# A three-stage fp32 trunk on one core: HGRN2's squares go into used-up keys, the last two features are made token-major by blocks, and the first weights are loaded ahead of x

## The chip, the cores and the metric

The kernel runs on one core of a Trainium2 chip. The time is that of the device for one execution, in microseconds; before the change it is 1544.46, the median of three runs (1542.48 to 1546.43). One execution was profiled; it took 1544.98. The engines are TensorE (PE: matrix products and transposes), VectorE (DVE), ScalarE (ACT), GpSimd (POOL) and SyncE (SP), which issues nearly all DMA transfers.

## The reference, cut to what matters

The input is x, 512 tokens of 1024 features in float32. Layer 0 mixes tokens with HGRN2 (8 heads of 128), layer 1 with Mamba-2 (a state-space mixer); each is followed by a gated convolutional feed-forward stage (2816 wide, "ConvGLU"). Every stage adds to a residual stream h, and a last RMSNorm ends it.

```python
def hgrn2_mixer(u, w_in, lb, norm_w, w_out):
    q, f_fw, f_bw, iv, g = jnp.split(u @ w_in, 5, axis=-1)
...
    o = gla_chunked(q, k_fw, iv, logf_fw) + flip(gla_chunked(flip(q), flip(k_bw), flip(iv), flip(logf_bw)))
    o = rmsnorm(o, norm_w) * jax.nn.silu(heads(g))
    return o.reshape(bsz, seq, HG_DIM) @ w_out
```

So the output of a head is normalised by the mean of its 128 squares per token, multiplied by a gate, and projected. The last line of the whole is rmsnorm(h, final_norm_w): for each token, the 1024 features divided by the root of their mean square, times a weight per feature.

## The kernel before

**Layout.** Nearly everything lies feature-major: 128 features on the partitions, 512 tokens along them; h is 8 such tiles. Weights come from memory in pieces of 128 x 4 x 256 floats (`load`, L123 to L131). `halves` (L133) splits each into a rounded half `whi`, cast by ScalarE (L137), and a rest `wlo`, subtracted by VectorE (L138); activations are split into `uhi`, `ulo` in the same way. `mm3` (L162) makes a product of high precision from three: hi x hi, hi x lo, lo x hi (L163 to L165). These triples are most of TensorE's work: 512 or 256 columns each, 128 x 128 stationary.

**HGRN2 (up to about 350 us).** The projections of the 8 heads, two heads at a time (`proj_pair`), and then the output projection are the "fill": a generator that reports how many units it has issued (a triple of 256 columns is about half a unit). `mix` (L544) is a head's attention, cut by `yield` into steps: five levels that both heads of a pair take together, then four steps for each head apart: transposes of keys (`kt`), states (`sd`, L653), output (`po`, L670), and transposes of the normalised output (L683). `weave` runs the fill and takes a step of a head when the fill has issued as many units as three tables say: a pair's start, its levels, and the ends of its first and second head, counted from the pair's start.

```python
PAIRS = (66, 138, 214, 289)
LEVELS = (0, 5, 18, 32, 45)
ENDS = ((50, 55, 62, 69), (56, 61, 68, 74))
```

That is TensorE's order, which is written out by hand. VectorE, ScalarE and GpSimd get theirs from a scheduler that places what is ready by the order of the program. Behind the output product stands a head's end, in the step L670 to L688: four squares on ScalarE with the sums of each row (L674, into `on`), the mean on VectorE (L675), a power on GpSimd (L677), four scalings on ScalarE (L679, `po` to `on`); in the last step four transposes on TensorE (L683), gate (L685, `on`), `yhi` on ScalarE, and `ylo` on VectorE (L687), the last reader of `on`. `on` has one buffer for all heads. `kq` holds a head's keys and queries, forward and backward, in four planes (KF, QB, QF, KB), in two buffers; the plane KF is last read by the transposes of the keys. The next pair's `kq`, its sum of keys (`km`, L596) and the gates F (L514) stand between these on VectorE; TensorE's first step of the next pair needs that `km` of both heads.

**The start (L327 on).** SyncE issues x in four pieces of 128 tokens and the first weights in turn. TensorE transposes each piece of x (L407), 8 transposes for each; between them, on ScalarE and VectorE, the first weights and the features are split.

**The end (`last_out`, L1109).** The last projection makes two feature tiles (256 features) from each of four pieces of weights, 10 triples of 512 columns for a tile; the last piece is done in two halves of 256 columns. `finish` adds the product to h, squares it and sums over the tiles, scales by the norm weight, and one tile later transposes 128 x 128 blocks to token-major `o`; after the last tile come the sums over features (`stats`, L223), a power on GpSimd (L234), the scaling of o by `rtok` on VectorE (L1132) and ScalarE, and two transfers for each block of 128 tokens (L1135).

## Time and profile before

| | |
|---|---|
| median of three runs | 1544.46 us |
| the profiled execution | 1544.98 us |
| its span in the trace | 1543.2 us |
| mean granted clock of TensorE, share of full | 0.995 |
| instructions | 24667 |
| busy: TensorE, VectorE, ScalarE, GpSimd | 99%, 67%, 51%, 2% |

The span is the time from the first to the last instruction that the profile shows; the execution's own time has 1.8 us around it. A granted clock of 1.00 is TensorE's upper level, 2.4 GHz; 0.50 is the lower, 1.2 GHz. A row of the timeline gives start, duration, engine, line, operation, tiles written and read, and in brackets how long the engine had been idle before and what ended that. TensorE's instructions overlap: one of 128 x 512 is shown at 0.39 us, and the next starts 0.23 us after it.

### The profile page before, as it was taken

To read this page: it belongs to the slowest core of one execution; us is meant where nothing else is said; L and a number is where in the kernel's file an instruction comes from. 1 tells how busy PE (TensorE), PEld (TensorE's weight loads), DVE (VectorE), ACT (ScalarE), POOL (GpSimd) and SP (SyncE) were. 2 spreads that over 40 slices of the span, in tenths; PEclk is the share of its full clock that TensorE was granted. 3 is DMA by queue.
4 is the path that set the end of the run, shared out by engine and by line. 5 is a ranking of instruction groups with operands and counts; after the bars stand their busy time and mean duration, and the time that the engine had idled before them with its cause. 6 is when DMAs were issued, how large, how long until landed. Compare 5 with 4: busy or idle time off the path is not lost.

```text
span 1543.2 us, 24667 instructions
## 1 busy us (share of the span) xinstructions
PE 1521.1 (99%) x9959; PEld 1289.5 (84%) x9959; DVE 1035.1 (67%) x1675; ACT 794.1 (51%) x1418; POOL 26.5 (2%) x31
## 2 busy tenths in 40 slices
PE   9999999999999999999999999999999999999998
PEld 7888888887888888888888888888888888888887
DVE  6887777748665346554999987788877665346542
ACT  5656555445433223333699888668745432223333
POOL 0000000000000000000000000000000000000000
PEclk9999999999999999999999999999999999999999
DMA  6321221113232233223454443343213232233221
GB/s 198 96 80 59 70 70 62 57 48 123 96 98 94 94 97 110 77 95 102 101 164 127 143 123 110 102 132 109 83 62 123 96 100 92 96 96 110 79 91 63
DMA packets 153593, 151.52 MB, mean 98 GB/s; under 512 B 8375, under 2 KB 144264, under 8 KB 153480
## 3 DMA queue, kind: packets, MB, share of 16 engines
q1 hardware_dynamic: 153415, 149.93, 31.2%
q8 instruction: 78, 1.28, 0.3%
q14 instruction: 36, 0.29, 0.1%
q0 software_dynamic: 32, 0.02, 0.0%
q10 hardware_dynamic: 32, 0.01, 0.0%
HBM read 147.70 MB, written 2.23 MB: 97 GB/s over the span
## 4 chain that ended last, share of the span: by engine, by line
PE 88%; ACT 4%; DVE 4%; DMA 2%; issue 1%; POOL 1%; SPq 0%; POOLq 0%; ACTq 0%; DVEq 0%
PE pp L163 25%; PE pp L164 25%; PE pp L165 25%; PE pm L165 1%; PE pm L163 1%; PE pm L164 1%; ACT E L952 1%; PE pm L561 1%; PE pm L974 1%; PE pm L1007 1%; PE pm L670 1%; PE pm L1022 1%; DVE wlo L138 1%; PE pm L653 1%; DMA raw<-in_b_w_in_dram 1%
## 5 line engine op out<-in xcount | busy, mean ns | idle before, releaser
L163 PE MATMUL pp<-uhi,whi 128*128 128x512 f32 x1136 | 450.6, 397 | 0.9 <-ACT sz L905 0.9
L165 PE MATMUL pp<-uhi,wlo 128*128 128x512 f32 x1136 | 443.0, 390 | 0.0
L164 PE MATMUL pp<-ulo,whi 128*128 128x512 f32 x1136 | 442.6, 390 | 0.0
L137 ACT CAST whi<-raw 128x1024 fp32r<-128x1024 f32 (+1 forms) x258 | 259.2, 1007 | 293.2 <-PE pp L164 223.7
L138 DVE TENSOR_TENSOR wlo<-raw,whi 128x1024 fp32r<-128x1024 f32 (+1 forms) x258 | 301.2, 1169 | 134.2 <-ACT whi L137 133.7
L163 PEld LDWEIGHTS pp<-uhi,whi 128*128 128x128 f32 x1136 | 213.6, 188 | 45.3 <-ACT sz L905 1.3
L165 PEld LDWEIGHTS pp<-uhi,wlo 128*128 128x128 f32 x1136 | 213.4, 188 | 45.6 <-DVE wlo L138 0.4
L164 PEld LDWEIGHTS pp<-ulo,whi 128*128 128x128 f32 x1136 | 213.7, 188 | 43.0 <-issue 0.2
L163 PE MATMUL pp<-yh,whi 128*128 128x512 f32 (+1 forms) x500 | 194.3, 389 | 0.0
L165 PE MATMUL pp<-yh,wlo 128*128 128x512 f32 (+1 forms) x500 | 190.6, 381 | 0.0
L164 PE MATMUL pp<-yl,whi 128*128 128x512 f32 (+1 forms) x500 | 190.4, 381 | 0.0
L163 PE MATMUL pp<-whi,uhi 128*128 128x256 f32 x384 | 112.2, 292 | 0.0
L164 PE MATMUL pp<-wlo,uhi 128*128 128x256 f32 x384 | 110.2, 287 | 0.0
L165 PE MATMUL pp<-whi,ulo 128*128 128x256 f32 x384 | 110.1, 287 | 0.0
L165 PEld LDWEIGHTS pp<-yh,wlo 128*128 128x128 f32 x500 | 94.0, 188 | 18.3
L163 PEld LDWEIGHTS pp<-yh,whi 128*128 128x128 f32 x500 | 94.0, 188 | 17.9 <-DVE h L268 0.3
L164 PEld LDWEIGHTS pp<-yl,whi 128*128 128x128 f32 x500 | 94.1, 188 | 17.4
L268 DVE TENSOR_TENSOR h<-h,pp 128x512 f32<-128x512 f32 x80 | 54.3, 684 | 79.8 <-PE pp L165 79.3
L952 ACT ACTIVATE E<-R,col_t 128x128 f32<-128x128 f32 x256 | 81.7, 394 | 7.2 <-DVE E L956 4.9
L727 ACT ACTIVATE c<-gp,colp 128x512 f32<-128x512 f32 x44 | 35.7, 816 | 89.8 <-DVE gp L725 89.8
L729 DVE SCALAR_TENSOR_TENSOR c<-gp,colp,c 128x512 f32<-128x512 f32 x88 | 65.6, 750 | 18.9 <-ACT c L727 17.5
L163 PEld LDWEIGHTS pp<-whi,uhi 128*128 128x128 f32 x384 | 75.4, 196 | 0.6
(281 smaller groups left out, 1974.9 us busy)
## 6 DMA issues: line engine op xcount, KB each, us to landing
raw<-in_ffn_w_in_dram SPq DMA_DIRECT2D x88, 512.0 KB, 3.5
raw<-in_a_w_in_dram SPq DMA_DIRECT2D x40, 512.0 KB, 3.6
raw<-in_ffn_w_out_dram SPq DMA_DIRECT2D x40, 512.0 KB, 3.4
raw<-in_b_w_in_dram SPq DMA_DIRECT2D x32, 512.0 KB, 4.0
R<-ac_d SPq DMA_DIRECT2D x64, 256.0 KB, 3.6
raw<-in_b_w_in_dram SPq DMA_DIRECT2D x32, 256.0 KB, 4.0
raw<-in_b_w_out_dram SPq DMA_DIRECT2D x12, 512.0 KB, 3.4
xt<-in_x_dram SPq DMA_DIRECT2D x4, 512.0 KB, 8.3
```

Source lines behind the costliest of these rows:

```text
L137: A.copy(hi[:, :nk, :c0], r)
L138: V.tensor_tensor(lo[:, :nk, :c0], r, hi[:, :nk, :c0].bitcast(F32), ALU.subtract)
L163: PE.matmul(dst, lhi, rhi, start=start, stop=False)
L164: PE.matmul(dst, lhi, rlo, start=False, stop=False)
L165: PE.matmul(dst, llo, rhi, start=False, stop=stop)
L268: V.tensor_tensor(h[d], h[d], p, ALU.add)
L561: PE.matmul(p[j:j + Q, b * Q:(b + 1) * Q], lhs(b * P + j), rhs(b * P + j), start=True, stop=True)
L653: PE.matmul(pl[:, n * P:(n + 1) * P], kt[dr][:, n * P:(n + 1) * P], v[:, b, i * P:(i + 1) * P], start=True, stop=True)
L670: PE.matmul(po[:, ts], l, r, start=n == 0, stop=n == len(parts) - 1)
L727: A.activation(c, g[:, 0:T], AF.Identity, scale=col(W_FW[l], f), bias=col(W_FB, l * NFF + f))
L729: V.scalar_tensor_tensor(c, g[:, k:k + T], col(W_FW[l], k * NFF + f), c, ALU.mult, ALU.add)
L952: A.activation(e[:, bs], r[:, bs], AF.Identity, bias=col_t[:, b, dr * NH + hd:dr * NH + hd + 1])
```

## The change

There are four edits. The table ENDS gives the first head's last two steps and the second head's last three earlier places (one or two units), so that two pairs of steps change places on TensorE. In `mix`, the squares are written into the plane KF of the head's own `kq`; only the scaling writes to `on`. At the start, the first weights are loaded ahead of x, and split ahead of the first transposed column table. And `last_out` makes the last two tiles in another way: for each block of 128 tokens the activations are the stationary side and 256 columns of weights are moved, so that the product comes out token-major; h of these two tiles is transposed into `o` at the beginning of the stage, the sums over the first six tiles are made ahead, and `close` ends each block by itself: add, squares with their sum per token, mean, power, scaling, two transfers. The last 256 norm weights are loaded over all partitions once (`wl`) by GpSimd.

```diff
--- before.py
+++ after.py
@@ -34,7 +34,7 @@
-ENDS = ((50, 55, 62, 69), (56, 61, 68, 74))
+ENDS = ((50, 55, 61, 67), (56, 61, 67, 74))
...
+    def sums():
         pst = misc_ps()
-        for b in blocks:
-            for n, s in enumerate((ssum, *more)):
-                for j in range(0, P, Q):
-                    PE.matmul(pst[j:j + Q, b:b + 1], s[:, b * P + j:b * P + j + Q], ones[:, 0:1],
-                              start=n == 0, stop=n == len(more))
-        bs = slice(blocks[0], blocks[-1] + 1)
+        for b in range(NB):
+            for j in range(0, P, Q):
+                PE.matmul(pst[j:j + Q, b:b + 1], ssum[:, b * P + j:b * P + j + Q], ones[:, 0:1], start=True, stop=True)
+        return pst
+
+    def stats(tmp):
+
+        pst = sums()
         ms = tmp.tile([P, NB], F32, tag="ms", name="ms", bufs=2)
-        V.tensor_scalar(ms[:, bs], pst[:, bs], 1.0 / D, EPS, ALU.mult, ALU.add)
-        G.tensor_tensor(rtok[:, bs], ms[:, bs], nhalf[:, bs], ALU.pow)
+        V.tensor_scalar(ms, pst[:, 0:NB], 1.0 / D, EPS, ALU.mult, ALU.add)
+        G.tensor_tensor(rtok, ms, nhalf, ALU.pow)
@@ -324,10 +323,10 @@
         nc.sync.dma_start(rows[r:r + n, g, :], src)
         return (g, r)
-    load_x(0)
     parts = [plan.popleft()[1] for _ in range(4)]
     raws = [None] * 4
     raws[0] = load(parts[0])
+    load_x(0)
     load_x(1)
     raws[2] = load(parts[2])
     load_x(2)
@@ -424,12 +423,12 @@
         for _ in range(16):
             PE.transpose(pt[:, P:2 * P], ident, ident)
         first_masks()
+        w = halves(*raws[0])
         PE.transpose(pt[:, :16], n1, ident[:16, :16])
         V.tensor_copy(coln, pt[:, :16])
         come(0, 1, 2, 3)
         split(0, W_N1, px[0])
         split(1, W_N1, px[1])
-        w = halves(*raws[0])
         first_products(0, 0, 2, w)
         stay(0, 1)
         come(4, 5)
@@ -668,10 +667,11 @@
                 parts += [(kq[:, a, ts], states[dr, t]) for dr, a in ((0, QF), (1, QB)) if (dr, t) in states]
                 for n, (l, r) in enumerate(parts):
                     PE.matmul(po[:, ts], l, r, start=n == 0, stop=n == len(parts) - 1)
-            on = t2k("on", 1)
+
+            on, sq = t2k("on", 1), kq[:, KF, :]
             ss = pool.tile([P, NB], F32, tag="ss", name="ss", bufs=2)
             for t in range(NB):
-                A.activation(on[:, t * P:(t + 1) * P], po[:, t * P:(t + 1) * P], AF.Square, accum_out=ss[:, t:t + 1])
+                A.activation(sq[:, t * P:(t + 1) * P], po[:, t * P:(t + 1) * P], AF.Square, accum_out=ss[:, t:t + 1])
             V.tensor_scalar(ss, ss, 1.0 / P, EPS, ALU.mult, ALU.add)
             rs = pool.tile([P, NB], F32, tag="rs", name="rs", bufs=2)
             G.tensor_tensor(rs, ss, nhalf, ALU.pow)
@@ -1109,50 +1109,74 @@
     def last_out(key, yhi, ylo, pool):
         o = [pool.tile([P, D], F32, tag="o", name="o", bufs=NB) for _ in range(NB)]
-        nk, po = len(yhi), [None]
-        def finish(d, p, ts, blocks):
-            V.tensor_tensor(h[d][:, ts], h[d][:, ts], p[:, ts], ALU.add)
-            sq = squares(d, pool, ts, d < ND - 1)
-            A.activation(h[d][:, ts], h[d][:, ts], AF.Copy, scale=col(W_FN, d))
+        wl = pool.tile([P, 256], F32, name="wl")
+        nc.gpsimd.dma_start(wl, final_norm_w[D - 256:D].rearrange("(a c) -> a c", a=1).to_broadcast([P, 256]))
+        nk, po, last = len(yhi), [None], 6
+        ms1, ms, sqt = (pool.tile([P, NB], F32, name=n) for n in ("ms1", "msl", "sqt"))
+        def finish(d, p):
+            V.tensor_tensor(h[d], h[d], p, ALU.add)
+            squares(d, pool)
+            A.activation(h[d], h[d], AF.Copy, scale=col(W_FN, d))
             to = po[0]
             yield
-            if d == ND - 1:
-                stats(pool, blocks, (sq,))
-            for b in blocks:
-                PE.transpose(to[b][:, d % 4 * P:(d % 4 + 1) * P], h[d][:, b * P:(b + 1) * P], ident)
-            if d == ND // 2 - 1:
-                for b in blocks:
-                    A.copy(o[b][:, 0:D // 2], to[b])
-            if d == ND - 1:
-                lo, hi = slice(0, D // 2), slice(D // 2, D)
-                for b in blocks:
-                    r = rtok[:, b:b + 1]
-                    V.tensor_scalar(o[b][:, lo], o[b][:, lo], r, None, ALU.mult)
-                    A.activation(o[b][:, hi], to[b], AF.Copy, scale=r)
-                    for ds in (lo, hi):
-                        nc.sync.dma_start(out[0, b * P:(b + 1) * P, ds], o[b][:, ds])
+            for b in range(NB):
+                t = to[b][:, d * P:(d + 1) * P] if d < 4 else to[b // 2][:, b % 2 * 256 + d % 2 * P:b % 2 * 256 + d % 2 * P + P]
+                PE.transpose(t, h[d][:, b * P:(b + 1) * P], ident)
+            if d == 3:
+                for b in range(NB):
+                    A.copy(o[b][:, 0:512], to[b])
+            if d == last - 1:
+                for b in range(NB):
+                    A.copy(o[b][:, 512:768], to[b // 2][:, b % 2 * 256:b % 2 * 256 + 256])
+                pst = sums()
+                V.tensor_scalar(ms1, pst[:, 0:NB], 1.0 / D, EPS, ALU.mult, ALU.add)
+        def close(b, p):
+            r, bs, hi = rtok[:, b:b + 1], slice(b, b + 1), o[b][:, 768:D]
+            V.tensor_tensor(hi, hi, p[:, 0:256], ALU.add)
+            sq = pool.tile([P, 256], F32, tag="sql", name="sql", bufs=2)
+            A.activation(sq, hi, AF.Square, accum_out=sqt[:, bs])
+            V.scalar_tensor_tensor(ms[:, bs], sqt[:, bs], 1.0 / D, ms1[:, bs], ALU.mult, ALU.add)
+            G.tensor_tensor(r, ms[:, bs], nhalf[:, bs], ALU.pow)
+            V.tensor_scalar(o[b][:, 0:512], o[b][:, 0:512], r, None, ALU.mult)
+            A.activation(o[b][:, 512:768], o[b][:, 512:768], AF.Copy, scale=r)
+            V.scalar_tensor_tensor(hi, hi, r, wl, ALU.mult, ALU.mult)
+            for ds in (slice(0, 512), slice(512, D)):
+                nc.sync.dma_start(out[0, b * P:(b + 1) * P, ds], o[b][:, ds])
         left = iter(())
         with tc.manual_schedule(engines={mybir.EngineType.PE}):
-            for c in range(4):
+            for b0 in (0, 2):
+                pt = misc_ps()
+                for b in (b0, b0 + 1):
+                    for i in range(2):
+                        t = (b - b0) * 256 + i * P
+                        PE.transpose(pt[:, t:t + P], h[last + i][:, b * P:(b + 1) * P], ident)
+                for b in (b0, b0 + 1):
+                    A.copy(o[b][:, 768:D], pt[:, (b - b0) * 256:(b - b0) * 256 + 256])
+            for c in range(3):
                 w = take((key, c))
-                if c % 2 == 0:
-                    po = [[misc_ps() for _ in range(NB)]]
-                for n in range(1 if c < 3 else 2):
-                    blocks = range(NB) if c < 3 else range(2 * n, 2 * n + 2)
-                    ts = slice(blocks[0] * P, (blocks[-1] + 1) * P)
-                    for i in range(2):
-                        p = proj_ps()
-                        for k in range(nk):
-                            mm3(p[:, ts], w(0, k, i * P), w(1, k, i * P), yhi[k][:, ts], ylo[k][:, ts],
-                                k == 0, k == nk - 1)
-                            if k == nk // 2:
-                                run(left)
-                        left = finish(2 * c + i, p, ts, blocks)
-                        next(left)
-            run(left)
+                if c != 1:
+                    po = [[misc_ps() for _ in range(NB if c == 0 else 2)]]
+                for i in range(2):
+                    p = proj_ps()
+                    for k in range(nk):
+                        mm3(p, w(0, k, i * P), w(1, k, i * P), yhi[k], ylo[k], k == 0, k == nk - 1)
+                        if k == nk // 2:
+                            run(left)
+                    left = finish(2 * c + i, p)
+                    next(left)
+            w = take((key, 3))
+            for b in range(NB):
+                bs = slice(b * P, (b + 1) * P)
+                p = proj_ps()
+                for k in range(nk):
+                    mm3(p[:, 0:256], yhi[k][:, bs], ylo[k][:, bs], w(0, k, 0, 256), w(1, k, 0, 256), k == 0, k == nk - 1)
+                    if k == nk // 2:
+                        run(left)
+                close(b, p)
     hgrn2()
     ffn(0, lambda key, yh, yl, pool: run(out_proj(key, yh, yl, lambda d: prep(d, (W_N1[0], W_N1[1] + 8), pool))))
```

On TensorE, around the end of the third pair (heads 4 and 5; `at_2425` is the first head's, `at_2436` the second's), before, from the first head's states to the second head's output:

```order
L653 MATMUL pm<-v,kt 128x128 x6
L670 MATMUL pm<-v,at_2425 128x128
...
L670 MATMUL pm<-v,at_2436 128x128
...
L165 MATMUL pp<-uhi_86,wlo 128x512
L683 MATMUL pm<-ident,on 128x128 x4
...
L165 MATMUL pp<-uhi_90,wlo 128x512
L683 MATMUL pm<-ident,on 128x128 x4
```

And now (lines have moved by one):

```order
L669 MATMUL pm<-v,at_2425 128x128
...
L652 MATMUL pm<-v,kt 128x128 x6
...
L165 MATMUL pp<-uhi_84,wlo 128x512
L683 MATMUL pm<-ident,on 128x128 x4
L669 MATMUL pm<-v,at_2436 128x128
...
L165 MATMUL pp<-uhi_90,wlo 128x512
L683 MATMUL pm<-ident,on 128x128 x4
```

Before, the second head's output stands ahead of the first head's transposes, with six products between them, and 12 products lie between the two sets of transposes. Now the first head's transposes come directly ahead of the second head's output, and 18 products lie between that and the second set; the first head's output comes ahead of the second head's states.

On VectorE, at the same place, before (`ss_3235` is the second head's sum of squares, `kq_3322` and `km_3329` are the next pair's second head's):

```order
L511 TENSOR_TENSOR pr_3281<-pp_3216,rbc_99 128x512
L138 TENSOR_TENSOR wlo_3295<-raw_3292,whi_3294 128x1024
L675 TENSOR_SCALAR ss_3235<-ss_3235 128x4
L514 TENSOR_SCALAR F_2954<-pr_3281,olb_107,lb_106 128x512
L552 TENSOR_TENSOR kq_3322<-q_2952,F_2954 128x512
L685 SCALAR_TENSOR_TENSOR on_3234<-pm_3273,colp_102,g_2775 128x512
L596 TENSOR_TENSOR km_3329<-kq_3322 128x512
L687 TENSOR_TENSOR ylo5_505<-on_3234,yhi5_497 128x512
```

And now (`ss_3243` and `on_3242` are the second head's):

```order
L675 TENSOR_SCALAR ss_3243<-ss_3243 128x4
...
L138 TENSOR_TENSOR wlo_3289<-raw_3286,whi_3288 128x1024
L685 SCALAR_TENSOR_TENSOR on_3242<-pm_3273,colp_102,g_2775 128x512
L510 TENSOR_TENSOR pr_3281<-pp_3216,rbc_99 128x512
L138 TENSOR_TENSOR wlo_3295<-raw_3292,whi_3294 128x1024
L687 TENSOR_TENSOR ylo5_505<-on_3242,yhi5_497 128x512
L513 TENSOR_SCALAR F_2954<-pr_3281,olb_107,lb_106 128x512
L551 TENSOR_TENSOR kq_3322<-q_2952,F_2954 128x512
L595 TENSOR_TENSOR km_3329<-kq_3322 128x512
```

The sum of squares stood behind both weight splits (`wlo_3295` is the second) and now stands ahead of both; the next pair's `km_3329` stood ahead of `ylo5` and now stands behind it, with both splits, `on_3242` and the gate's product between the sum and it.

On SyncE, the first transfers before:

```order
L320 DMA xt<-in_x_dram 128x4x256
L129 DMA raw<-in_a_w_in_dram 128x4x256
L320 DMA xt<-in_x_dram 128x4x256
L129 DMA raw<-in_a_w_in_dram 128x4x256
L320 DMA xt<-in_x_dram 128x4x256 x2
```

And now:

```order
L129 DMA raw<-in_a_w_in_dram 128x4x256
L319 DMA xt<-in_x_dram 128x4x256 x2
L129 DMA raw<-in_a_w_in_dram 128x4x256
L319 DMA xt<-in_x_dram 128x4x256 x2
L129 DMA raw<-in_a_w_in_dram 128x4x256
```

The first piece of weights stands ahead of the first piece of x; the second piece of x is third in both.

## Rows read from the trace of the kernel before

**Rows 1.** The page: its head, the busy times of the engines, and the shares of the chain that ended last.

```profile
span 1543.2 us, 24667 instructions
...
PE 1521.1 (99%) x9959; PEld 1289.5 (84%) x9959; DVE 1035.1 (67%) x1675; ACT 794.1 (51%) x1418; POOL 26.5 (2%) x31
...
PE 88%; ACT 4%; DVE 4%; DMA 2%; issue 1%; POOL 1%; SPq 0%; POOLq 0%; ACTq 0%; DVEq 0%
```

**Rows 2.** TensorE's waits: tile and line that waited, what ended the wait, us in total, times, the longest.

```profile
PE pm L683 <- ACT on L679: 10.1, 4, 3.8
```

**Rows 3.** The timeline of TensorE, with start and duration: an undisturbed stretch first, then the second heads' transposes of the first three pairs, each with the product before and behind it.

```profile
122.34 0.28 PE L165 MATMUL pp<-whi,ulo 128*128 128x256 f32 x1
122.81 0.36 PE L163 MATMUL pp<-whi,uhi 128*128 128x256 f32 x1
...
125.65 0.28 PE L165 MATMUL pp<-whi,ulo 128*128 128x256 f32 x1
128.42 1.10 PE L683 MATMUL pm<-ident,on 128*128 128x128 f32 x4 [2.49 <-ACT on L679]
129.28 0.36 PE L163 MATMUL pp<-whi,uhi 128*128 128x256 f32 x1
...
194.43 0.28 PE L165 MATMUL pp<-whi,ulo 128*128 128x256 f32 x1
197.58 1.10 PE L683 MATMUL pm<-ident,on 128*128 128x128 f32 x4 [2.87 <-ACT on L679]
198.44 0.36 PE L163 MATMUL pp<-whi,uhi 128*128 128x256 f32 x1
...
267.88 0.39 PE L165 MATMUL pp<-uhi,wlo 128*128 128x512 f32 x1
272.05 1.25 PE L683 MATMUL pm<-ident,on 128*128 128x128 f32 x4 [3.78 <-ACT on L679]
272.95 0.56 PE L163 MATMUL pp<-whi,uhi 128*128 128x256 f32 x1
```

**Rows 4.** TensorE by stretches: the stretch, sum of busy time, busy time with the number of instructions, granted clock, share and GB/s of DMA. Second and third pair.

```profile
199.00:202.42 3.42, 3.42 (x19) 0.50 0.00 0
202.42:205.84 3.42, 3.42 (x29) 1.00 0.00 0
270.68:277.51 6.83, 5.46 (x25) 0.50 0.24 79
```

**Rows 5.** The third pair. From the timelines of TensorE, ScalarE and GpSimd: first head's states, its output, the product behind it; the product behind the second head's output; the first of the second head's squares, its power and its scaling. Then groups of VectorE from 255 to 276 us by line: busy us, mean ns of one, idle time before them.

```profile
253.62 1.50 PE L653 MATMUL pm<-v,kt 128*128 128x128 f32 x12
254.95 0.39 PE L670 MATMUL pm<-v,at 128*128 128x128 f32 x2
257.11 0.48 PE L163 MATMUL pp<-uhi,whi 128*128 128x512 f32 x1
263.45 0.48 PE L163 MATMUL pp<-uhi,whi 128*128 128x512 f32 x1
269.03 0.27 ACT L674 ACTIVATE on<-pm 128x128 f32<-128x128 f32 x1
270.58 1.01 POOL L677 TENSOR_TENSOR rs<-ss,nhalf 128x4 f32<-128x4 f32 x1 [10.53 <-DVE ss L675]
271.63 1.14 ACT L679 ACTIVATE on<-pm,rs 128x128 f32<-128x128 f32 x4 [0.94 <-POOL rs L677]
...
L685 DVE SCALAR_TENSOR_TENSOR on<-pm,colp,g 128x512 f32<-128x512 f32 x2 | 1.5, 747 | 1.3 <-PE pm L683 1.3
L687 DVE TENSOR_TENSOR ylo<-on,yhi 128x512 fp32r<-128x512 f32 x2 | 1.4, 688 | 0.1
L514 DVE TENSOR_SCALAR F<-pr,olb,lb 128x512 f32<-128x512 f32 x2 | 1.1, 546 | 1.2 <-ACT pr L512 1.2
```

**Rows 6.** The start: TensorE's timeline, the first weight cast on ScalarE and the first split on VectorE, and a stretch by engines (PE, PEld, DVE, ACT, POOL, then granted clock and DMA).

```profile
4.98 1.09 PE L407 MATMUL pm<-ident,xt 128*128 128x128 f32 x8
7.80 1.95 PE L407 MATMUL pm<-ident,xt 128*128 128x128 f32 x8 [1.73 <-DMA xt<-in_x_dram]
9.40 0.78 PE L163 MATMUL pp<-uhi,whi 128*128 128x512 f32 x1
6.83 1.04 ACT L137 CAST whi<-raw 128x1024 fp32r<-128x1024 f32 x1
7.90 1.23 DVE L138 TENSOR_TENSOR wlo<-raw,whi 128x1024 fp32r<-128x1024 f32 x1
7.86:11.27 3.41, 3.41 (x13) 3.02 (x14) 3.37 (x5) 2.18 (x4) 0.00 (x0) 0.50 1.11 350
```

**Rows 7.** The end, the timeline of all engines: the last product, the add, the squares, the power, the first scaling, and the transfers' issue.

```profile
1534.86 0.28 PE L165 MATMUL pp<-yh,wlo 128*128 128x256 f32 x1
1535.18 0.42 DVE L1116 TENSOR_TENSOR h<-h,pp 128x256 f32<-128x256 f32 x1 [2.41 <-PE pp L165]
1535.63 0.42 ACT L218 ACTIVATE sq<-h 128x256 f32<-128x256 f32 x1 [2.78 <-DVE h L1116]
1536.78 0.70 POOL L234 TENSOR_TENSOR rtok<-ms,nhalf 128x2 f32<-128x2 f32 x1 [6.18 <-DVE ms L233]
1537.51 0.88 DVE L1132 TENSOR_SCALAR o<-o,rtok 128x512 f32<-128x512 f32 x2 [0.81 <-POOL rtok L234]
1538.03 1.79 SPq L1135 DMA_DIRECT2D out_dram<-o  x4
```

More of the change, by code (lines that the diff above doesn't have):

```diff
@@ L211, in split, with squares @@
         V.scalar_tensor_tensor(ulo[d], src, col(w, d), uhi[d].bitcast(F32), ALU.mult, ALU.subtract)
-    def squares(d, tmp, ts=slice(0, T), add=True):
+    def squares(d, tmp):
         if d == 0:
-            A.activation(ssum[:, ts], h[d][:, ts], AF.Square)
+            A.activation(ssum, h[d], AF.Square)
         else:
             sq = tmp.tile([P, T], F32, tag="pr", name="sq", bufs=2)
-            A.activation(sq[:, ts], h[d][:, ts], AF.Square)
-            if not add:
-                return sq
-            V.tensor_tensor(ssum[:, ts], ssum[:, ts], sq[:, ts], ALU.add)
-    def stats(tmp, blocks=range(NB), more=()):
-        pst = misc_ps()
-        for b in blocks:
-            for n, s in enumerate((ssum, *more)):
-                for j in range(0, P, Q):
-                    PE.matmul(pst[j:j + Q, b:b + 1], s[:, b * P + j:b * P + j + Q], ones[:, 0:1],
-                              start=n == 0, stop=n == len(more))
-        bs = slice(blocks[0], blocks[-1] + 1)
+            A.activation(sq, h[d], AF.Square)
+            V.tensor_tensor(ssum, ssum, sq, ALU.add)
+    def sums():
+        pst = misc_ps()
+        for b in range(NB):
[4 more added lines that the diff above has]
+        pst = sums()
         ms = tmp.tile([P, NB], F32, tag="ms", name="ms", bufs=2)
-        V.tensor_scalar(ms[:, bs], pst[:, bs], 1.0 / D, EPS, ALU.mult, ALU.add)
-        G.tensor_tensor(rtok[:, bs], ms[:, bs], nhalf[:, bs], ALU.pow)
+        V.tensor_scalar(ms, pst[:, 0:NB], 1.0 / D, EPS, ALU.mult, ALU.add)
+        G.tensor_tensor(rtok, ms, nhalf, ALU.pow)
     def diagonals(tmp):
```

## The prediction

> **What bounds the kernel now.** I read the page first, then TensorE's list of waits, then the timeline around each long wait, then the table of stretches with the granted clock, and last the first ten and the last nine microseconds. On the page the reader is to see that TensorE is busy for 99% of the span and holds 88% of the chain that ended last [rows 1]. So nothing that saves work on another engine counts by itself: time is won where TensorE waits, where it runs below its full clock, or at the two ends. The list of waits says where it waits: 10.1 of some 16 us of idle time are four waits for `on` in the HGRN2 stage [rows 2], and 1.7 us is the wait for x at the start [rows 6]. Those four are the second head of each pair of heads; the first heads' transposes cost nothing extra.
>
> The timeline gives their real price. Undisturbed, from the product before the four transposes to the product behind them is 0.47 us (122.34 to 122.81); after a product of 512 columns, which takes 0.23 instead of 0.12, it is 0.58. In the first three pairs it is 3.63, 4.01 and 5.07 us [rows 3]. That is 3.16, 3.54 and 4.49 us too much, 11.2 together; the fourth wait, 0.9 us in the list, I take at 1.2 with the slower pace of its transposes, as the others cost a little more than their idle time. Sum 12.4.
>
> The waits have a second price. After the second and the third, the granted clock is 0.50 (1.2 GHz) for 3.42 and 6.83 us, then 1.00 again [rows 4]. In the first of these stretches 19 products fit where the next stretch of equal length has 29: ten products at 0.118 us, 1.2 us, or half of 3.42, 1.7, at most; I take 1.4. In the second, the products run from 272.95 to 277.51, and the same share of 4.56 us is 1.9. Sum 3.3.
>
> **HGRN2: squares and order.** Before, the squares of a head's output are written into `on`, which has one buffer, so the second head's squares wait until `ylo` of the first has read it: in the third pair its output is done at 263.4, its squares begin at 269.03. Behind them stand the power on GpSimd (1.01) and the scaling (four in 1.14), then the transposes [rows 3, 5]. After, the squares go into the head's own keys, whose last reader is long done; only the scaling still needs `on`. No instruction is added or removed here. ENDS moves the first head's transposes ahead of the second head's output, and the first head's output ahead of the second head's states.
>
> I walk through the third pair with the rows' durations. Head one: output from 253.62 (2.16 us, the distance of 254.95 and 257.11), then the states (1.33), then 18 products (4.2); its transposes are due at 261.3. Its chain from 255.8: squares 1.1, power 1.0, scaling 1.14, some 0.4 of hand-overs, ready at 259.5 [rows 5]. No wait, 1.8 us to spare. Head two: transposes until 261.8, output until 263.9. ScalarE still copies the next pair's keys until about 264.4; squares until 265.5; VectorE, with the next pair's totals, reaches their sum at 266.1; power until 267.2, scaling 267.3 to 268.4. TensorE wants it at 263.9 + 4.2 = 268.1: 0.2 us of wait for the last quarter. The second pair, walked in the same way, waits 0.25; the first and last pairs, with no weights to split in between, nothing. So 0.45 remains.
>
> What is late next: the keys of the next pair. In the new order of VectorE, between the second head's sum of squares and the keys of the next pair's second head (`km_3329`) stand two weight splits (1.23 each) [rows 6], `on` times gate (0.75), `ylo` (0.69), the gate F (0.55), and the gate's product, the query and the keys, which have `ylo`'s form and are taken at its 0.69 [rows 5]. The first split waits for a ScalarE cast (1.04 in [rows 6]), which stands behind the scaling: 268.4 + 1.04 = 269.45, and 6.5 us of VectorE, 6.1 with the usual overlap of neighbours, end at 275.6. TensorE comes to it after 36 products of 256 columns: 268.6 + 4.3 + 0.6 for the first head's small products = 273.5. That is a new wait of about 2.0 us; the long wait and the half clock hid it before. Behind the first pair (24 products) the gate F is long done, and the keys are ready 1.5 us early; behind the second, 48 products leave 1.5 us. So HGRN2 gives 12.4 + 3.3 - 0.45 - 2.0 = 13.2.
>
> Of the clock: the two drops in the rows follow idle times of 2.87 and 3.78 us, and none follows the first pair's 2.49 [rows 3, 4]. I therefore take no drop after a wait of 2.0. The Trainium skill (TensorE: Matmul & The Clock Gate, "What's actually happening") puts the low rate as the default that activity lifts; the trace agrees, with 0.50 after idle stretches and 1.00 in between. By that rule alone a wait that stays would bring the low level back.
>
> **The end.** The last two feature groups are now made token-major, four blocks of 30 products with 256 columns, as many and as long as the 4 x 30 before. The eight transposes of those features go to the head of the stage, six of them from inside this window; 32 small matmuls for the sums become 16. TensorE's last product therefore ends where it did, within 0.2. Behind it before: add 0.42, squares 0.42, sums and mean until the power at 1536.78 (0.70), scaling from 1537.51 for two blocks on two engines, and four transfers from 1538.03, issued over 1.79 us; from the last product's start (1534.86) to the span's end 8.3 us [rows 7, 1]. After: add 0.3 + 0.42, squares with read-out 0.6, mean 0.2, power 0.8, at 2.35; VectorE then does the left 512 (0.44) and the right 256 columns (some 0.4), so the transfers are issued at 2.9 and 3.35, two of them instead of four. Four of 256 KB took as long as their bytes, some 0.67 each; two end at about 5.05, and 1.6 us follow as before: 6.65. Gain 1.7. The GpSimd load of the norm weights stands ahead of the stage's products and is hidden by those of the first six features, 180 of 0.23, some 41 us; without that cover it would hold up only the first block's close.
>
> **The start.** Weights, x0, x1 instead of x0, weights, x1. Before, x0 is there by 4.98 and x1 at 7.80, two transfers in 2.8, so 1.4 each [rows 6]. After, x0 comes at about 6.4, x1, third in both, at 7.8. The order of TensorE is unchanged: the first eight transposes fill the wait of 1.73, the next eight start at 7.80, and the products behind them. The weight split, which ran from 6.83 to 9.1, is now earlier, but `coln` stands behind it on VectorE, and the first `ulo` is done at 8.9, before the product that needs it (after 9.4). I take 0. Ends: 1.0 lost, if x0 lands no earlier than x1 and eight transposes are late; 1.7 won, if the clock stays up in the 3.41 us that run at 0.50 now [rows 6].
>
> **Sum.** 13.2 + 1.7 + 0 = 14.9. Against the profiled execution: 1544.98 (span 1543.2 and 1.8 around it) - 14.9 = 1530.1. That execution is 0.5 above the median 1544.46, so for the median 1529.6.
>
> **The rivals.** *The clock falls again.* The wait for the keys is longer than 2.0, or falls so that the level drops once or twice: 1.4 to 1.9 for each drop and 1 us of wait, about 1533. For it: three idle times near the border in these rows; against it: nothing between 50 and 360 us ran low without a wait near 3 us [rows 4].
> *No wait is left.* VectorE's neighbours overlap more, the keys are in time (2.4 back) and the start gains a little: 1526.5. For it: I let ScalarE's cast stand idle for its place; against: the order is fixed in the program.
> *The wait only moves.* The first head's scaling is late, TensorE stands before its transposes with the second head's output queued behind them, and what the second head gains the first head loses; only the end's 1.7 and a little remain: 1541. Against: 1.8 us to spare above.
> *Slower.* The squares hold the keys' buffer longer, so at each of the four pairs the next keys are late as well, and shorter but more frequent waits at three places of a pair leave the clock low for 6.8 us four times: 13.6 instead of 3.3 lost, waits as before, end 1.7 won: +8.6, about 1553. It decides from the point where the stretches at 0.50 in HGRN2 are longer than some 30 us in all. Nothing but the drops in [rows 4] speaks for it.
>
> **How the numbers follow.** Forecast 0.54; clock falls again 0.22; no wait left 0.14; wait only moves 0.07; slower 0.03. Range: the first three, with the start's ends, from 1525 to 1535.5. About 0.3%, 4.6 us, can be told from no change: faster than 1539.8 are the first three and a part of the fourth, 0.92; within 0.05; slower than 1549.1, 0.03.
>
> **What would show it.** TensorE's waits for `on` fall from 10.1 to under 1 us, with a new wait for `km` of about 2 us after the third pair; no stretch at 0.50 between 50 and 360 us; the span from the last product to the end 6.6 instead of 8.3; the first product of the projections still at about 9.4. I am wrong in the main step if waits for `on` of more than 3 us are left, or if the clock still drops after the second pair; wrong in the walk if the new wait is absent or stands behind another pair.

## The result, and the profile after

The changed kernel takes 1529.24 us (median of four runs, 1529.03 to 1529.94) against 1545.4 for the kernel before on the same chip: a ratio of 0.9902, 95% interval [0.9889, 0.9914]. The forecast was 1529.6, in a range of 1525 to 1535.5. The profiled execution took 1529.33 and has a span of 1527.5, 15.7 less than [rows 1].

The page of the changed kernel, its head, busy times and the shares of the chain that ended last:

```profile
span 1527.5 us, 24622 instructions
...
PE 1515.4 (99%) x9927; PEld 1285.8 (84%) x9927; DVE 1035.6 (68%) x1680; ACT 793.9 (52%) x1426; POOL 29.3 (2%) x34
...
PE 94%; ACT 3%; DVE 1%; DMA 1%; issue 1%; POOL 0%; SPq 0%; POOLq 0%; DVEq 0%; ACTq 0%
```

TensorE's busy time fell by 5.7 only; 10 us are idle time that is gone, and its share of the chain rose from 88 to 94%. TensorE's waits (total, times, longest), to be read against [rows 2]:

```profile
PE pm L406 <- DMA xt<-in_x_dram: 1.7, 2, 1.3
PE pm L560 <- DVE km L595: 1.6, 1, 1.6
...
PE pp L163 <- ACT sz L905: 0.9, 1, 0.9
PE pm L683 <- ACT on L679: 0.2, 1, 0.2
```

The waits for `on` fell from 10.1 to 0.2. One new wait stands there, for the next pair's `km`. The stretches by engine with the granted clock (length, busy time and count of PE, PEld, DVE, ACT and POOL, then PEclk, DMA share and GB/s) show one stretch at 0.50 ahead of the end, at the start, and none behind the new wait:

```profile
8.40:11.81 3.41, 3.41 (x14) 2.93 (x13) 3.41 (x6) 2.73 (x4) 0.00 (x0) 0.50 1.10 349
11.81:15.22 3.41, 3.41 (x21) 2.91 (x20) 3.18 (x5) 1.18 (x3) 0.00 (x0) 1.00 0.54 163
...
268.00:272.00 4.00, 3.15 (x84) 3.09 (x85) 4.00 (x9) 3.12 (x8) 0.00 (x0) 1.00 0.32 109
```

The two of [rows 4] are gone. The new wait, on the timelines of ScalarE, VectorE and TensorE behind the third pair (start, duration, and in brackets the idle time before with what ended it):

```profile
260.62 1.14 ACT L679 ACTIVATE on<-pm,rs 128x128 f32<-128x128 f32 x4 [1.18 <-POOL rs L677]
261.63 2.01 ACT L137 CAST whi<-raw 128x1024 fp32r<-128x1024 f32 x2
...
262.73 1.23 DVE L138 TENSOR_TENSOR wlo<-raw,whi 128x1024 fp32r<-128x1024 f32 x1 [1.91 <-ACT whi L137]
...
265.13 1.22 DVE L138 TENSOR_TENSOR wlo<-raw,whi 128x1024 fp32r<-128x1024 f32 x1
266.26 0.69 DVE L687 TENSOR_TENSOR ylo<-on,yhi 128x512 fp32r<-128x512 f32 x1
266.86 0.54 DVE L513 TENSOR_SCALAR F<-pr,olb,lb 128x512 f32<-128x512 f32 x1
267.44 0.69 DVE L551 TENSOR_TENSOR kq<-q,F 128x512 f32<-128x512 f32 x1
268.10 0.69 DVE L595 TENSOR_TENSOR km<-kq 128x512 f32<-128x512 f32 x1
...
268.85 0.46 PE L560 MATMUL pm<-q,km 128*32 128x32 f32 x32 [1.63 <-DVE km L595]
```

The reader is to see a chain: both weight casts stand behind the scaling on ScalarE, VectorE stands idle for 1.91 until the first is there, and from then on it has no gap until `km`, which TensorE has wanted since 267.2. The end, to be read against [rows 7]:

```profile
1521.04 0.28 PE L165 MATMUL pp<-whi,yl 128*128 128x256 f32 x1
1521.36 0.42 DVE L1138 TENSOR_TENSOR o<-o,pp 128x256 f32<-128x256 f32 x1 [0.85 <-PE pp L165]
1521.87 0.42 ACT L1140 ACTIVATE sql<-o 128x256 f32<-128x256 f32 x1 [1.73 <-DVE o L1138]
...
1522.65 0.54 POOL L1142 TENSOR_TENSOR rtok<-msl,nhalf 128x1 f32<-128x1 f32 x1 [3.05 <-DVE msl L1141]
...
1523.63 0.48 DVE L1145 SCALAR_TENSOR_TENSOR o<-o,rtok,wl 128x256 f32<-128x256 f32 x1
1523.75 0.81 SPq L1147 DMA_DIRECT2D out_dram<-o  x2
```

From the last product's start to the end of the span it is 6.5 us; before it was 8.3.

Later runs, which have the labels e1 to e12, are compared by sections of their one profiled execution, since a run's total mixes them. From the timelines, in us: the start of the 48th product of the projections (**start**); from there to the first instruction of Mamba's line L923 (**middle**: HGRN2 and the first feed-forward stage); from there to the last of L1022 (**Mamba**); from there to the start of the last product (**late**); from there to the end (**end**). For the two kernels:

| | start | middle | Mamba | late | end |
|---|---|---|---|---|---|
| before | 22.86 | 742.20 | 374.48 | 395.32 | 8.32 |
| changed | 23.13 | 728.68 | 373.62 | 395.62 | 6.47 |

### The profile page after: what moved, and what is told of

Read it like the earlier page. It is cut to its first block, busy times and chain, and to the rows that moved or that the text cites. A ratio compares the mean times of both kernels' runs of the same rounds, so it can differ in the third digit from the quotient of the medians.

```text
span 1527.5 us, 24622 instructions
## 1 busy us (share of the span) xinstructions
PE 1515.4 (99%) x9927; PEld 1285.8 (84%) x9927; DVE 1035.6 (68%) x1680; ACT 793.9 (52%) x1426; POOL 29.3 (2%) x34
## 4 chain that ended last, share of the span: by engine, by line
PE 94%; ACT 3%; DVE 1%; DMA 1%; issue 1%; POOL 0%; SPq 0%; POOLq 0%; DVEq 0%; ACTq 0%
PE pp L163 27%; PE pp L165 27%; PE pp L164 27%; PE pm L163 1%; PE pm L165 1%; PE pm L164 1%; PE pm L974 1%; PE pm L1007 1%; PE pm L669 1%; PE pm L560 1%; PE pm L1022 1%; PE pm L652 1%; ACT E L952 1%; DMA xt<-in_x_dram 0%; PE pm L923 0%
## 5 line engine op out<-in xcount | busy, mean ns | idle before, releaser
L163 PE MATMUL pp<-yh,whi 128*128 128x512 f32 x460 | 182.7, 397 | 0.0
L165 PE MATMUL pp<-yh,wlo 128*128 128x512 f32 x460 | 179.3, 390 | 0.0
L164 PE MATMUL pp<-yl,whi 128*128 128x512 f32 x460 | 179.1, 389 | 0.0
L165 PEld LDWEIGHTS pp<-yh,wlo 128*128 128x128 f32 x460 | 86.3, 188 | 18.3
L163 PEld LDWEIGHTS pp<-yh,whi 128*128 128x128 f32 x460 | 86.4, 188 | 17.7 <-DVE h L267 0.3
L164 PEld LDWEIGHTS pp<-yl,whi 128*128 128x128 f32 x460 | 86.4, 188 | 17.4
```

Source lines behind the costliest of these rows:

```text
L163: PE.matmul(dst, lhi, rhi, start=start, stop=False)
L164: PE.matmul(dst, lhi, rlo, start=False, stop=False)
L165: PE.matmul(dst, llo, rhi, start=False, stop=stop)
```

## The experiments

### Either edit of HGRN2 alone, the start alone, the end alone

Four kernels, each with one part of the change put into the kernel before.

**The squares alone (e1):**

```diff
-            on = t2k("on", 1)
+            on, sq = t2k("on", 1), kq[:, KF, :]
...
-                A.activation(on[:, t * P:(t + 1) * P], po[:, t * P:(t + 1) * P], AF.Square, accum_out=ss[:, t:t + 1])
+                A.activation(sq[:, t * P:(t + 1) * P], po[:, t * P:(t + 1) * P], AF.Square, accum_out=ss[:, t:t + 1])
```

> The kernel before with the squares in the keys' plane, and nothing else (old ENDS, start and end). Theory A (the one buffer `on` made the waits; the squares were its first user, and their move is enough): the scaling still needs `on`, which is free when the first head's ylo is done, by the trace of before at 268.4 in the third pair where the transposes are due at 268.1, and at 194.5 where they are due at 194.7. TensorE waits for `on` about 1.0, 0.3, 0 and 0: under 2 us of 10.1 are left, no drop of the clock in HGRN2, and 1531.5 to 1534.5. Theory B (the new places of the steps were needed: as long as the first head's ylo comes late, the second head's scaling is as late as its squares were): 5 us or more of the 10.1 are left, with at least one drop, 1537 to 1541.

Measured: 1533.47 against 1544.18, ratio 0.9939 [0.9922, 0.9955]; middle 730.95. TensorE's waits for `on` are 3.5, between the two theories; the time and the clock (no drop) are those of A, and there is no wait for `km`. In the third pair, from the timelines of VectorE, ScalarE and TensorE:

```profile
263.21 0.68 DVE L687 TENSOR_TENSOR ylo<-on,yhi 128x512 fp32r<-128x512 f32 x1
...
263.99 1.14 ACT L679 ACTIVATE on<-pm,rs 128x128 f32<-128x128 f32 x4 [0.21 <-DVE tot L591]
264.41 0.84 PE L683 MATMUL pm<-ident,on 128*128 128x128 f32 x3 [1.49 <-ACT on L679]
```

`ylo` ends at 263.89, and the scaling begins 0.1 behind it: it waits for `on`, although the label in brackets names another instruction of the same engine. The squares are free, the buffer still is not.

**The table alone (e2).** Of the second head only one place moves (68 to 67), not three as the section on the change has it:

```diff
-ENDS = ((50, 55, 62, 69), (56, 61, 68, 74))
+ENDS = ((50, 55, 61, 67), (56, 61, 67, 74))
```

> The kernel before with the new table ENDS, and nothing else (squares in `on`). Theory A (the wait was for the buffer; the new table alone frees it early, since the first head's ylo is then done before or about when the second head's output ends: in the trace of after at 257.98 against squares from 257.64 in the third pair, 189.11 against 188.29 in the second): waits for `on` of 0.3 to 1 in the second and third pair, under 2 us in all, no drop, a wait for km near 1.6 behind the third pair as in after, 1531.5 to 1534.5; then either edit does nearly all of it, and their gains do not add. Theory B (the move of the squares is what pays, the table only moves steps): 5 us or more of waits for `on` left, 1537 to 1543.

Measured: 1528.95 against 1544.18, ratio 0.9909 [0.9894, 0.9924], with the old start and the old end; middle 727.18. One line of the kernel takes all that the whole change takes; the time lies 2.5 below the range of theory A. TensorE's waits:

```profile
PE pm L407 <- DMA xt<-in_x_dram: 1.1, 1, 1.1
PE pp L163 <- ACT sz L905: 0.9, 1, 0.9
...
PE pm L683 <- ACT on L679: 0.3, 1, 0.3
```

Theory B falls. So does a part of A: there is no wait for `km`. ScalarE and VectorE at that place, to be read against the chain of the changed kernel above:

```profile
258.16 1.07 ACT L137 CAST whi<-raw 128x1024 fp32r<-128x1024 f32 x1
259.98 1.14 ACT L679 ACTIVATE on<-pm,rs 128x128 f32<-128x128 f32 x4 [0.74 <-POOL rs L677]
260.99 1.06 ACT L137 CAST whi<-raw 128x1024 fp32r<-128x1024 f32 x1
...
259.49 1.22 DVE L138 TENSOR_TENSOR wlo<-raw,whi 128x1024 fp32r<-128x1024 f32 x1
...
265.19 0.69 DVE L596 TENSOR_TENSOR km<-kq 128x512 f32<-128x512 f32 x1
```

Here a cast stands between the squares and the scaling, in the time in which ScalarE waits for GpSimd's power anyway; in the changed kernel the next pair's keys stand there, and both casts come behind. The first split begins at 259.49 instead of 262.73, and `km` is done at 265.88 instead of 268.79; 0.64 of either difference is only that the place itself lies earlier there (the transposes start at 260.40 instead of 261.04).

**The start alone (e3)** (weights loaded and split ahead of x):

```diff
-    load_x(0)
     parts = [plan.popleft()[1] for _ in range(4)]
...
     raws[0] = load(parts[0])
+    load_x(0)
...
+        w = halves(*raws[0])
         PE.transpose(pt[:, :16], n1, ident[:16, :16])
...
-        w = halves(*raws[0])
         first_products(0, 0, 2, w)
```

> The kernel before with the first weights loaded and split ahead of x, and nothing else. Theory A (the prediction): nothing, within 0.3 us of before in the same run; first product at 9.4 to 9.5, two short waits for x in place of one. Rival: the small losses in the trace of after (first product 0.09 late, 0.28 by the sixth product) stand: 0.3 us slower. Rival: the first waits are shorter and the stretch at 0.50 goes: 1.5 faster.

Measured: 1544.63 against 1544.18, ratio 1.0 [0.9991, 1.001], first product at 9.20. The third theory falls (3.41 us at 0.50 from 8.5 on are there); the first two can't be told apart by this.

**The end alone (e4)** (`last_out` of the diff, with `sums`; of it the closing of a block):

```diff
-            if d == ND - 1:
-                stats(pool, blocks, (sq,))
...
+        def close(b, p):
+            r, bs, hi = rtok[:, b:b + 1], slice(b, b + 1), o[b][:, 768:D]
+            V.tensor_tensor(hi, hi, p[:, 0:256], ALU.add)
...
+            for ds in (slice(0, 512), slice(512, D)):
+                nc.sync.dma_start(out[0, b * P:(b + 1) * P, ds], o[b][:, ds])
```

> The kernel before with the new last_out alone (old table, squares in `on`, old start). Theory A: from the last product's start to the end of the span 6.5 instead of 8.3, and 0.3 to 0.7 lost at the head of the stage for the eight transposes that come there: 1.1 to 1.5 faster, 1544.0 when before is 1545.4. Rival: the last transfers bound it, and half of it is given back: 0.5 or less.

Measured: 1542.2 against 1544.18, ratio 0.999 [0.998, 0.9999]; late 395.62 (0.30 more), end 6.47 (1.85 less). That is 1.55 net by the sections, theory A, and 2.0 by the medians; the loss at the head of the stage is the smallest that I allowed for.

### With and without each edit, on one chip

The changed kernel again (e5); without its edit of the start (e6); with the squares in `on` again (e7); and without both (e8, the new table and the new end alone).

**The changed kernel again (e5):**

> The changed kernel once more, as the measure for the next three: 1529.2, with a wait for km of 1.6 behind the third pair and a stretch at 0.50 of 3.41 us at the start.

Measured: 1529.71 (1528.48 to 1530.28), wait for `km` 1.64. The clock didn't do as expected: no low stretch at the start, but one behind the wait for `km`, where the first profile of this kernel had none:

```profile
265.40:268.88 3.48, 1.84 (x131) 1.53 (x130) 3.45 (x8) 1.65 (x4) 0.00 (x0) 1.00 0.45 151
268.88:272.30 3.42, 3.42 (x17) 3.42 (x18) 3.38 (x7) 2.21 (x5) 0.00 (x0) 0.50 0.03 5
272.30:275.72 3.42, 3.42 (x30) 3.42 (x30) 1.68 (x3) 2.00 (x5) 0.00 (x0) 1.00 0.00 0
```

17 products in place of 30, and a middle of 730.22 instead of 728.68: 1.54 us.

**Without the edit of the start (e6):**

```diff
+    load_x(0)
     parts = [plan.popleft()[1] for _ in range(4)]
...
-    load_x(0)
     load_x(1)
...
-        w = halves(*raws[0])
         PE.transpose(pt[:, :16], n1, ident[:16, :16])
...
+        w = halves(*raws[0])
         first_products(0, 0, 2, w)
```

> The changed kernel without its edit of the start (x0 loaded first again). Theory A (the prediction): the start is worth nothing, 1529.0 to 1529.4. Theory B (two looks with the edit had first a wait for x of 1.2 to 1.3 and then one of 0.4 and a stretch at 0.50 behind them, three of four without it had one wait of 0.9 to 1.1 and none): the edit costs half of a 0.50 stretch's products, 0.5 us or a little more: 1528.4 to 1528.8, first product at 9.0 to 9.1, no stretch at 0.50 at the start.

Measured: 1528.99 (1528.83 to 1530.74), first product at 8.85, no low stretch at the start, wait for `km` 1.64, middle 728.67. By its medians 0.7 faster than with the edit, but the ranges overlap.

**With the squares in `on` again (e7):**

```diff
-            on, sq = t2k("on", 1), kq[:, KF, :]
+            on = t2k("on", 1)
...
-                A.activation(sq[:, t * P:(t + 1) * P], po[:, t * P:(t + 1) * P], AF.Square, accum_out=ss[:, t:t + 1])
+                A.activation(on[:, t * P:(t + 1) * P], po[:, t * P:(t + 1) * P], AF.Square, accum_out=ss[:, t:t + 1])
```

> The changed kernel with the squares in `on` again (new ENDS, start and end kept). Theory A (the move of the squares costs: since they no longer wait for `on`, the scheduler puts the next pair's keys, not a weight cast, between squares and scaling on ScalarE, and both casts behind it; the next keys' wait of 1.6 comes from that): no wait for km, waits for `on` 0.3 more, 1527.4 to 1527.9. Theory B (the wait for km comes from the new table, and the run with the table alone missed it by its start): 1529 to 1529.5, wait for km 1.3 to 2.0.

Measured: 1528.05 (1526.48 to 1528.44), middle 727.26, no wait for `km`, 0.3 of waits for `on`. All of TensorE's waits:

```profile
PE pm L406 <- DMA xt<-in_x_dram: 2.2, 2, 1.6
PE pm L424 <- POOL ident masks.py:199: 1.5, 1, 1.5
PE pp L163 <- ACT sz L905: 0.9, 1, 0.9
PE pm L683 <- ACT on L679: 0.3, 1, 0.3
```

Theory A: with the new table, the move of the squares costs 1.4 us of the middle, and 3.0 where the clock falls with it. The time is 0.15 over the range given.

**Without both (e8):**

> The new ENDS and the new end alone: squares in `on`, old start. The table alone gave 1528.95; the end's 1.84 behind the last product, less 0.25 that its transposes cost ahead of it, make 1527.0 to 1527.5, 2 under the changed kernel, if the parts add. If the end's gain needs the rest: 1528.5 or more.

Measured: 1528.52 (1527.45 to 1528.85), middle 727.28, late 395.67, end 6.47. The middle is again that of the table alone. The total lies just inside the second range, but late and end are what the first one was built on; the Mamba stage, which no edit touches, took 374.57, 0.8 more than in the run of the table alone.

### What makes the next keys late

**The squares in a tile of their own (e9)**, with the old start (`bfloat16`, 128 x 128; the sums stay float32):

```diff
-            on, sq = t2k("on", 1), kq[:, KF, :]
+            on, sq = t2k("on", 1), pool.tile([P, P], mybir.dt.bfloat16, tag="sqx", name="sqx", bufs=1)
...
-                A.activation(sq[:, t * P:(t + 1) * P], po[:, t * P:(t + 1) * P], AF.Square, accum_out=ss[:, t:t + 1])
+                A.activation(sq, po[:, t * P:(t + 1) * P], AF.Square, accum_out=ss[:, t:t + 1])
```

> The changed kernel with the old start, and the squares written to a small tile of their own (128 x 128 in bfloat16, all four to the same place; the sums stay float32), neither to `on` nor to the keys. On ScalarE a weight cast then stands between the second head's squares and its scaling in the third pair, as with the squares in `on`. Theory A (the wait for km comes from the place of that cast, not from which tile holds the squares): no wait for km over 0.5, waits for `on` under 0.6, 1527.0 to 1528.0. Theory B (the squares begin early because they don't wait for `on`, and their early begin pushes the next keys back): wait for km of 1.0 to 2.0, 1528.6 to 1529.4.

Measured: 1532.58, middle 732.25, slower than either theory allowed. TensorE's longest waits:

```profile
PE pm L683 <- ACT on L679: 3.3, 2, 2.0
PE pm L406 <- DMA xt<-in_x_dram: 1.7, 1, 1.7
```

No wait for `km`, as A has it, but 3.3 of waits for `on`, which neither theory has. Since the four squares write one place, the scheduler put other work between them; the cast came ahead of the last square instead of behind it, so that sum, power and scaling were late by the cast. Behind the longer of the two waits the granted clock fell to 0.50 for 3.41 us. The run shows that a cast ahead of the sum brings waits for `on` back; it does not single out which tile's use moves the next keys. That the place of the cast causes the wait for `km` rests on the rows of the two kernels above, on e7, and on the next run; no run moves that cast alone.

**The fourth pair two units later (e10)**, the squares in the keys, the old start:

```diff
-PAIRS = (66, 138, 214, 289)
+PAIRS = (66, 138, 214, 291)
```

> The changed kernel with the old start and PAIRS = (66, 138, 214, 291): the squares stay in the keys, and the fourth pair's first products come 12 products of 256 columns later, 1.44 us. Theory A (the keys are ready at a time that VectorE's order sets, and TensorE only comes too early): the wait for km falls from 1.64 to 0.2, the fourth pair's end has no new wait, 1527.3 to 1528.0. Theory B (the keys' order follows the later steps, so the wait moves with them): 1.2 or more is left. Theory C (the fourth pair's end, moved by as much, runs into the end of the fill and waits): a wait for `on` of 1 or more at 330 us, 1528.8 or more.

Measured: 1527.88 (1527.01 to 1528.35), ratio 0.9892 [0.9875, 0.9908]; middle 727.24, 1.43 less than without it. TensorE at that place:

```profile
267.72 0.46 PE L560 MATMUL pm<-q,km 128*32 128x32 f32 x32 [0.20 <-DVE km L595]
```

Theory A, with its number: the keys come when VectorE's order brings them, and 12 products put ahead of the step fill the wait.

### The end on top of the table

**The table alone again (e11):**

> The new table alone once more, as the measure for the next: 1528.95 as before, 8.31 from the last product's start to the end.

Measured: 1528.34 (1528.17 to 1529.73), end 8.30, middle 727.22.

**The table and the new end (e12, the kernel of e8):**

> The new table and the new end, beside the table alone on the same chip. Theory A (the traces: 0.33 more ahead of the last product, 1.84 less behind it): 1.5 below the run beside it. Rival (the earlier pair of runs, 1528.95 and 1528.52, on different chips): 0.4 below.

Measured: 1527.98 (1527.47 to 1528.49), late 395.64 against 395.28, end 6.47 against 8.30: 1.47 in the sections, but 0.36 by the medians. Of the rest, 0.46 stands in Mamba (373.93 against 373.47) in the two profiles. The time around the span differs a little too: 1.7 to 1.8 us in the runs of the table alone, 1.9 to 2.1 in these. It is 1.8 to 2.1 in every run of the six kernels with the new end and the old start, and 1.7 to 1.8 in those with both new; the runs do not show why. So the net of the end is 1.5 by the sections, 0.4 by these medians, whose ranges overlap, and 2.0 by those of e4; what it is within these bounds stays open.

## Why the prediction was right, and where not

**What bounds it.** Right: TensorE's waits and the clock behind them made the time. The middle fell by 13.5; 13.2 were forecast for HGRN2 (12.4 of waits, 3.3 of clock, less 0.45 and 2.0 that stay). The waits for `on` that I let stay are there in kind: 0.15 of idle time in the third pair where 0.2 were said, and in the second, where 0.25 were said, the transposes only run slower, 1.08 instead of 0.60. Their size was too small. From TensorE's timeline of the changed kernel, the second and the third pair, with the power on GpSimd:

```profile
191.52 0.28 PE L165 MATMUL pp<-whi,ulo 128*128 128x256 f32 x1
191.64 1.08 PE L683 MATMUL pm<-ident,on 128*128 128x128 f32 x4
192.47 0.36 PE L163 MATMUL pp<-whi,uhi 128*128 128x256 f32 x1
...
260.50 0.39 PE L165 MATMUL pp<-uhi,wlo 128*128 128x512 f32 x1
261.04 1.10 PE L683 MATMUL pm<-ident,on 128*128 128x128 f32 x4 [0.15 <-ACT on L679]
261.90 0.36 PE L163 MATMUL pp<-whi,uhi 128*128 128x256 f32 x1
...
259.20 1.38 POOL L677 TENSOR_TENSOR rs<-ss,nhalf 128x4 f32<-128x4 f32 x1 [7.62 <-DVE ss L675]
```

Counted as the prediction counted the old waits, from the product before to the product behind, these places still cost 0.48 and 0.82, together 1.3 where 0.45 was taken. The power took 1.38 in both, where 1.01 was taken from [rows 5]; the runs do not show why. That the middle still fell by the forecast amount is in part luck: the wait for `km` was 0.4 shorter than said, and a wait of 0.41 for a `wlo` at 358 us, which the kernel before has, is gone too, which I had not counted.

**The new wait.** Right in its place (behind the third pair alone), in its cause (two splits, `on` times gate, the product, `ylo`, F, query and keys, one behind the other) and nearly in its size: 2.0 said, 1.63 measured. VectorE took 6.06 from the first split to the end of `km` where I had 6.1, and began as soon as the first cast was done. The delay by 1.44 in e10 removes it to 0.20.

**The squares.** Here the step failed that the total could not test. I put "Before, the squares of a head's output are written into `on`" as the cause and walked both edits as one. The runs show two edits that free the same buffer from its two ends. The table lets the first head give `on` back before the second head needs it (middle 742.20 to 727.18), the move of the squares lets the second head's squares go without it (to 730.95), and both together (728.68) are not better than the table alone but 1.5 worse. The gain is not a sum: on top of the squares the table still wins 2.3 (0.7 in e5, where the clock falls), but on top of the table the squares win nothing and cost the place of a cast on ScalarE and with it the wait for `km`. I had seen that wait and booked it on "the new order"; it takes the squares on top of the table, since neither the table alone (e2) nor the squares alone (e1) has it.

**The clock.** Right in the main: the two low stretches of [rows 4] go with the long waits. "I therefore take no drop after a wait of 2.0" was half a matter of luck: with waits of 1.63, 1.64 and 1.64 at the same place in three profiles (changed, e5, e6) the level fell in one. By the Trainium skill (TensorE: Matmul & The Clock Gate, "What's actually happening") the low level is the default and activity lifts it. The one profile agrees with that; the other two show that a wait of this size does not bring the low level each time. So the first rival, given 0.22, is not another outcome but a part of this kernel's runs. 1.5 us is its price, as [rows 4] gave it; the time of that execution is 1530.28, not the 1533 of the rival.

**The end.** 1.7 forecast, 1.85 measured behind the last product. The power on one column took 0.54, not 0.8, and the transfers were issued from 1523.75 on, 2.7 behind the last product's start, where I had 2.9. That the last product "ends where it did, within 0.2" was off by a little: late is 395.62 to 395.67 in every kernel with the new end, 395.28 to 395.32 in every one without it. Net 1.55 by the sections; by medians of runs 0.4 (e12) to 2.0 (e4).

**The start.** Forecast 0. In the four profiles with the edit (changed, e3, e5, e7) the first product starts at 9.20 to 10.03, in the ten without it at 8.85 to 9.40. With it TensorE waits 1.2 to 1.6 for x0, which comes behind the weights, and in three of the four 0.4 to 0.7 again for x1; without it there is one wait, 0.8 to 1.7 for x1, and in six of the ten 0.3 to 0.5 for the first `wlo`. A stretch at 0.50 of 3.41 us follows in three of the four (all but e5) and in two of the ten (before, e9); the section start is 22.86 to 23.22 with such a stretch and 21.68 to 22.43 without one. That speaks for a loss of some 0.5 to 1, in the direction of the bound that I had set at 1.0. Three pairs of kernels, each on one chip, give +0.45 (e3 against before), +0.7 (e5 against e6) and -0.5 (e7 against e8) by medians, so that it stays open.

**The sum.** 14.9 forecast, 15.66 by the spans: middle 13.52, end 1.85 and late -0.30, start -0.27, and 0.86 in Mamba. Mamba is between 373.4 and 374.6 over all 14 profiles, and two of the same kernel (e8, e12) differ by 0.64, so I take this last term as spread and no effect; without it the sum is 14.8. Of the other rivals, "the wait only moves" and "slower" fell: no wait takes the place of the old one at the first head, and nothing in the keys' buffer makes pairs late. "No wait is left" is nearly what the table alone does.

The best of these, the change with the squares kept in `on` (with either start), or with the fourth pair two units later and the old start, take 1527.9 to 1528.5, 1 us or so below the changed kernel. The ranges overlap a little; the middle (727.2 to 727.3 in their profiles against 728.67 to 730.22 in those of the changed kernel, e5 and e6) tells them apart.

## What to carry to other kernels

If two edits free the same buffer, walk each alone, and each on top of the other, before adding them. Here the second won less than alone or nothing, and one of them cost 1.4 on top of the other, as far as the rows show because a cast came later in a scheduled queue. Try a table of due times first: three numbers of it took nearly all of the wait without any memory. A second buffer for `on` was not run. And compare kernels section by section between fixed instructions: the middle repeats within 0.1 us as long as the clock does not fall, where the totals of one such kernel differ by up to 2.

## What the runs showed of the hardware that was not expected

After waits of the same length at the same place the granted clock falls in some executions and not in others. At the second heads' transposes, after 2.49 us of idle time, it fell in one of three profiles (in e4, not in before and e3); after 2.87 and 3.78 in each of the three; after 2.01 in the one of e9; after the 1.6 for `km` in one of three; after the 1.0, 1.0 and 1.5 of e1 and the 1.3 of e9 not at all. Behind one wait of 1.55 to 1.73 at the start it fell in two of four (before, e9, not e6 and e10). It stayed low for 3.41 us, or for 6.83 after the longest wait in two of three profiles. TensorE in the stretch behind the 2.49 of e4 and the 2.01 of e9:

```profile
129.76:133.17 3.41, 3.41 (x18) 0.50 0.01 2
...
195.93:199.34 3.41, 3.41 (x18) 0.50 0.00 0
```

The spread of the kernel before goes with this: 1542.1 to 1547.6 over 19 runs, with mean granted clocks of 0.996 and 0.992 at these ends, while the changed kernel's eight runs lie within 1528.5 and 1530.3.
